# A decoder block in hi/lo fp32r: matmuls of the row-wise products and the classical projections in another loop order

## The chip, the cores and the metric

The kernel runs on one core of a Trainium2 chip. Times are device microseconds (us) of whole executions; the kernel before took 2509.76 us, the median of three (2505.5 to 2514.46). The profile is of one execution on the same core. Its engines are TensorE (PE; the loading of a matmul's stationary operand is shown apart, as PEld), VectorE (DVE), ScalarE (ACT), GpSimd (POOL) and SyncE (SP); all run their own instruction streams in a fixed order and wait for each other by semaphores.

## The reference

One layer of a decoder, 512 tokens of width 2048, all in float32. What matters here are its matrix products:

```python
h = rmsnorm(x, g_mix[l])
z = jnp.einsum('bsd,dc->bsc', h, w_in[l])
cb, cc, cv, q, k, v, f_logit, gate_c, gate_a = jnp.split(z, SPLIT_POINTS, axis=-1)
conv_branch = jnp.einsum('bsc,cd->bsd', cb * causal_dwconv(cc * cv, conv_w[l]), w_conv_out[l])
...                                  # attn: forgetting attention of q, k, v
attn_branch = jnp.einsum('bsc,cd->bsd', attn, w_attn_out[l])
merged = gc * conv_branch + ga * attn_branch        # gates: sigmoids of z's last columns
x = x + jnp.einsum('bsd,de->bse', merged, w_mix_out[l])
h = rmsnorm(x, g_mlp[l])
u = jnp.square(jax.nn.relu(jnp.einsum('bsd,df->bsf', h, w_ff1[l])))
x = x + jnp.einsum('bsf,fd->bsd', u, w_ff2[l])
return rmsnorm(x, g_final)
```

The widths: conv and attention 1024 each, the MLP 8192 (FF1: 2048 to 8192, FF2: 8192 to 2048).

## The kernel before

**Numbers.** Each float32 operand of a large product is written as hi + lo, both of type fp32r, which TensorE reads in one pass. A product is three matmuls, hi x hi, hi x lo and lo x hi. Activations are split once and kept. Weights are split as they come: `split` (L99 to L101) makes the hi part on ScalarE (L100, tile `th`) and the lo part as source minus hi on VectorE (L101, tile `tl`). `th` and `tl` have two buffers each, so that a third `th` can only be written when the matmuls that read the first are through.

**Seven products.** The projections of w_in, FF1 and FF2 cut both operands in 2 x 2 blocks and form seven products (A11, A12, S4, S2, S3, S1, A22) instead of eight, from sums and differences of blocks; these are made by `sub` (L104) and `add` (L107) on VectorE. One product, called a piece here, is a chain of matmuls that accumulate in PSUM. There are two helpers for a piece. `mm_cols` (L126) has the weights as stationary and the tokens as moving operand (FF1, the gates, conv and k/q columns); it isn't touched. `mm_rows` (L148) has the activations as stationary operand `Sx(q)` (hi and lo) and the weights' `hi`, `lo` as the moving one. Its result is two blocks of 128 tokens, b = 0 and 1, in two PSUM banks (for the 256 columns of `gV0`, the two halves of one). It is used by the v heads (`gV0`, `gV1`) and by FF2.

**FF2** is `unit` (L957): 8 segments of the 8192 rows times 2 column groups, so 16 units, each of 7 pieces of 24 matmuls 128x512 (4 values of q, 2 blocks, 3 matmuls). Four weight tiles are loaded, called y00, y01, y11, y10. The pieces come in the order A11 (y00), S3, S2, A22, S1, A12, S4. In between VectorE makes y00 = y01 - y00 and y01 = y11 - y01 (the operand of S3), t2 = y11 - y00 (of S2), t2 = y10 - t2 (of A22); and `into` adds each finished result into `x1` (L107; in the last segment the final result goes through `finish`, L938 and L941, and `residual`, L951). The PSUM tiles a and d change places from one unit to the next.

**The classical projections** are not cut in that way. `gemm_t` (L294) has weights as stationary operand, four result tiles of 128 columns in four banks, and is called for w_conv_out and w_attn_out for each of four column groups; its `consume` (L652 and following) multiplies by the gates and splits the merged sum. `gemm_n` (L315) has tokens stationary and makes w_mix_out; per token tile three matmuls by `mm3` (L310); its `consume` adds the residual (L107) and squares it (L337). Both take the weights in chunks of 4 x 128 rows by `wchunk`, and consume the results after the last chunk.

**What sets the order.** No order is written out by hand: a scheduler takes the program in the order of the code with its dependencies and decides, when the kernel is built, in which order each engine gets its instructions. So a turned loop on TensorE can also shift instructions of VectorE and ScalarE against each other.

In time, the v heads and k/q columns lie up to 277 us, the attention with conv columns up to 505, the gates up to 880, gemm_t from 880 to 1054, gemm_n to 1234, FF1 to 1861, FF2 to 2491, and the last normalisation to 2503.7.

Of the kernel before, what the change touches and what calls it, by code (L numbers as in the profile page):

```python
# [15 lines left out]
P = 128  # L16
# [29 lines left out]
def tile_hybrid_block(ctx: ExitStack, tc, x, g_mix, w_in, b_f, b_gate, conv_w, w_conv_out,  # L46
                      w_attn_out, w_mix_out, g_mlp, w_ff1, w_ff2, g_final, out):
    nc = tc.nc
# [99 lines left out]
    def mm_rows(ps, Sx, hi, lo, first):  # L148

        nq, w = hi.shape[1], hi.shape[2]  # L150
        for b in range(2):
            o = ps[b][:, :w] if len(ps) == 2 else ps[0][:, b * w:(b + 1) * w]
            begin = first and (b == 0 or len(ps) == 2)
            ts = slice(b * P, (b + 1) * P)
            for part in range(2):
                for q in range(nq):
                    Sh, Sl = (e[:, ts] for e in Sx(q))
                    if part == 0:
                        nc.tensor.matmul(o, Sh, hi[:, q, :], start=begin and q == 0, stop=False, skip_group_check=True)  # L159
                        nc.tensor.matmul(o, Sl, hi[:, q, :], start=False, stop=False, skip_group_check=True)  # L160
                    else:
                        nc.tensor.matmul(o, Sh, lo[:, q, :], start=False, stop=q == nq - 1, skip_group_check=True)  # L162

    def moving(t):

# [128 lines left out]
    def gemm_t(view, kt, c0, act, banks, consume, slots=(0, 3, 2)):  # L294

        ps = [bank(i, "pt") for i in banks]
        for k0 in range(0, kt, 4):
            hi, lo = wchunk(view, k0, c0, slot(slots))
            for j in range(4):
                js = slice(j * P, (j + 1) * P)  # L300
                for q in range(4):
                    k = k0 + q
                    xh, xl = act(k)
                    nc.tensor.matmul(ps[j], hi[:, q, js], xh, start=k == 0, stop=False)  # L304
                    nc.tensor.matmul(ps[j], hi[:, q, js], xl, start=False, stop=False)  # L305
                    nc.tensor.matmul(ps[j], lo[:, q, js], xh, start=False, stop=k == kt - 1)
        for j in range(4):
            consume(j, ps[j])

# [5 lines left out]
    def gemm_n(view, kt, c0, act, banks, consume, toks=range(NT), slots=(0, 3, 2), between={}):  # L315

        ps = {t: bank(i, "pn") for t, i in zip(toks, banks)}
        for k0 in range(0, kt, 4):
            hi, lo = wchunk(view, k0, c0, slot(slots))
            for t in toks:  # L320
                for q in range(4):
                    xh, xl = act(k0 + q, t)
                    mm3(ps[t], xh, xl, hi[:, q, :], lo[:, q, :], k0 + q == 0, k0 + q == kt - 1)
            between.get(k0 // 4, lambda: None)()
        for t in toks:
            consume(t, ps[t])
# [754 lines left out]
```

## Time and profile before

| what | value |
|---|---|
| runs | 2505.5, 2509.76, 2514.46 us |
| profiled execution, first to last instruction (span) | 2503.7 us |
| mean granted TensorE clock | 0.996 |
| busy: PE, PEld, DVE, ACT, POOL | 2446.6, 2249.2, 1902.1, 1150.3, 112.7 us |
| matmuls in the profile | 16910 |

The profile shows no own time of its execution beside the span: the span is what a reader compares with the runs, which lie 1.8 to 10.8 us above it, the median 6.1. A matmul's busy time overlaps with the next one's (a 128x512 matmul is shown with 0.39 us), so that the step from one start to the next, not the duration, is what a matmul costs. In a row of a group or of the timeline, `a<-th,us 128*128 128x512` is the result tile, the moving operand and the stationary one, the stationary's shape, and the moving operand's shape. In brackets stands the idle time before an instruction and what ended it. In the rows of stretches come the stretch, its length, each engine's busy time with the number of its instructions, the granted clock, the DMA share and GB/s.

### The profile page before, as it was taken

The page shows a single profiled execution, that of the slowest core. Times are in us where ns is not written, and L with a number is a line of the kernel's source. Part 1 is how long each engine was busy: PE and PEld are TensorE (multiplying, and loading weights), DVE is VectorE, ACT ScalarE, POOL GpSimd, SP SyncE. Part 2 cuts the span into 40 slices and gives each one's busy share as a digit, 9 for nine tenths or more (in the row PEclk, how much of TensorE's full clock was granted, in tenths as well). Part 3 has the DMA queues.
Part 4 walks back from the last instruction along what each step waited for, and adds up shares of the span by engine and source line. Part 5 has one row for each costly group of instructions (what it writes and reads, how often), then busy time and mean ns, then how long its engine had stood idle before and what let it go on. Part 6 is the DMA issues. An engine that isn't in the chain of part 4 may idle for free.

```text
span 2503.7 us, 39010 instructions
## 1 busy us (share of the span) xinstructions
PE 2446.6 (98%) x16910; PEld 2249.2 (90%) x16910; DVE 1902.1 (76%) x1498; ACT 1150.3 (46%) x1136; POOL 112.7 (5%) x184
## 2 busy tenths in 40 slices
PE   7999999999999999999999999999999999999997
PEld 7999989999999988888899999999998878787785
DVE  7877677788777743535688898898887887878888
ACT  6443433434544622235655666666664333333343
POOL 0000000000000000000000000000011000000010
PEclk9999999999999999999999999999999999999999
DMA  7554444456544544435655655646688557664573
GB/s 240 165 170 156 151 135 148 143 179 209 157 134 131 189 161 151 141 121 197 210 172 180 238 178 202 241 174 217 224 308 281 162 189 239 212 215 157 187 259 105
DMA packets 289919, 465.06 MB, mean 186 GB/s; under 512 B 10236, under 2 KB 194644, under 8 KB 289620
## 3 DMA queue, kind: packets, MB, share of 16 engines
q1 hardware_dynamic: 260704, 330.40, 41.1%
q0 software_dynamic: 28176, 131.08, 14.0%
q8 instruction: 132, 2.16, 0.4%
q10 hardware_dynamic: 868, 1.10, 0.1%
q14 instruction: 39, 0.32, 0.0%
HBM read 370.26 MB, written 92.27 MB: 185 GB/s over the span
## 4 chain that ended last, share of the span: by engine, by line
PE 67%; DVE 10%; ACT 3%; DMA 2%; issue 2%; POOL 0%; SPq 0%; ACTq 0%; POOLq 0%; DVEq 0%
PE a L142 5%; PE a L146 5%; PE a L144 5%; PE d L142 3%; PE d L144 3%; PE d L146 3%; DVE tl L101 3%; ACT th L100 3%; PE a L159 3%; PE a L160 3%; PE a L162 3%; PE pt L304 2%; PE pt L305 2%; PE pn L311 2%; PE pn L312 2%; PE pn L313 2%
## 5 line engine op out<-in xcount | busy, mean ns | idle before, releaser
L101 DVE TENSOR_TENSOR tl<-x,th 128x2048 fp32r<-128x2048 f32 (+1 forms) x252 | 575.1, 2288 | 211.0 <-ACT th L100 194.5
L100 ACT ACTIVATE th<-x 128x2048 fp32r<-128x2048 f32 (+1 forms) x252 | 482.4, 1917 | 484.9 <-PE a L144 171.3
L104 DVE TENSOR_TENSOR x<-x,x 128x2048 f32<-128x2048 f32 (+1 forms) x144 | 329.2, 2286 | 17.0 <-DMA x<-in_w_ff_dram 9.3
L100 ACT ACTIVATE th<-y 128x2048 fp32r<-128x2048 f32 x80 | 153.7, 1921 | 271.8 <-DVE y L104 102.6
L101 DVE TENSOR_TENSOR tl<-y,th 128x2048 fp32r<-128x2048 f32 x80 | 182.7, 2284 | 47.4 <-ACT th L100 47.4
L101 DVE TENSOR_TENSOR tl<-raw,th 128x2048 fp32r<-128x2048 f32 x40 | 91.7, 2293 | 151.9 <-ACT th L100 151.4
L159 PE MATMUL a<-th,us 128*128 128x512 f32 x512 | 200.8, 392 | 2.5 <-ACT o L864 1.5
L160 PE MATMUL a<-th,us 128*128 128x512 f32 x512 | 199.4, 389 | 0.0
L142 PE MATMUL a<-ST,th 128*128 128x256 f32 x768 | 178.7, 278 | 8.5 <-ACT th L100 8.5
L144 PE MATMUL a<-ST,th 128*128 128x256 f32 x768 | 178.1, 278 | 0.0
L100 ACT ACTIVATE th<-raw 128x2048 fp32r<-128x2048 f32 x40 | 76.7, 1918 | 175.4 <-PE pt L305 71.5
L142 PEld LDWEIGHTS a<-ST,th 128*128 128x128 f32 x768 | 145.3, 189 | 9.4 <-ACT th L100 9.3
L144 PEld LDWEIGHTS a<-ST,th 128*128 128x128 f32 x768 | 145.3, 189 | 0.0
L142 PE MATMUL a<-S,th 128*128 128x256 f32 x576 | 134.6, 279 | 5.0 <-ACT th L100 5.0
L162 PE MATMUL a<-tl,us 128*128 128x512 f32 x512 | 136.9, 389 | 0.1
L144 PE MATMUL a<-S,th 128*128 128x256 f32 x576 | 134.0, 278 | 0.0
L159 PEld LDWEIGHTS a<-th,us 128*128 128x128 f32 x512 | 96.1, 188 | 27.5 <-ACT th L100 6.1
L142 PE MATMUL d<-ST,th 128*128 128x256 f32 x512 | 117.7, 276 | 0.0
L144 PE MATMUL d<-ST,th 128*128 128x256 f32 x512 | 117.7, 276 | 0.0
L162 PEld LDWEIGHTS a<-tl,us 128*128 128x128 f32 x512 | 95.9, 188 | 20.7 <-DVE tl L101 0.9
L142 PEld LDWEIGHTS a<-S,th 128*128 128x128 f32 x576 | 108.3, 188 | 6.3 <-ACT th L100 6.0
L160 PEld LDWEIGHTS a<-th,us 128*128 128x128 f32 x512 | 96.1, 188 | 19.6
(284 smaller groups left out, 6232.4 us busy)
## 6 DMA issues: line engine op xcount, KB each, us to landing
x<-in_w_in_dram SPq DMA_DIRECT2D x86, 1024.0 KB, 5.8
x<-in_w_ff_dram SPq DMA_DIRECT2D x66, 1024.0 KB, 8.3
y<-in_w_ff_dram SPq DMA_DIRECT2D x64, 1024.0 KB, 6.3
us<-s_d POOLq DMA_DIRECT2D x48, 1024.0 KB, 8.8
s_d<-rh POOLq DMA_DIRECT2D x32, 896.0 KB, 5.3
s_d<-r POOLq DMA_DIRECT2D x32, 896.0 KB, 8.0
raw<-in_w_mix_out_dram SPq DMA_DIRECT2D x24, 1024.0 KB, 5.1
g_d<-o SPq DMA_DIRECT2D x32, 256.0 KB, 2.2
```

The costliest lines, as they stand in the source:

```text
L100: nc.scalar.activation(out=hi, in_=src, func=AF.Copy)
L101: nc.vector.tensor_tensor(out=lo, in0=src, in1=hi.bitcast(F32), op=ALU.subtract)
L104: nc.vector.tensor_tensor(out=out, in0=a, in1=b, op=ALU.subtract)
L142: nc.tensor.matmul(o, hi[:, q, js], Sh, start=first and q == 0 and j == 0, stop=False, skip_group_check=True)
L144: nc.tensor.matmul(o, hi[:, q, js], Sl, start=False, stop=False, skip_group_check=True)
L146: nc.tensor.matmul(o, lo[:, q, js], Sh, start=False, stop=q == nq - 1, skip_group_check=True)
L159: nc.tensor.matmul(o, Sh, hi[:, q, :], start=begin and q == 0, stop=False, skip_group_check=True)
L160: nc.tensor.matmul(o, Sl, hi[:, q, :], start=False, stop=False, skip_group_check=True)
L162: nc.tensor.matmul(o, Sh, lo[:, q, :], start=False, stop=q == nq - 1, skip_group_check=True)
L304: nc.tensor.matmul(ps[j], hi[:, q, js], xh, start=k == 0, stop=False)
L305: nc.tensor.matmul(ps[j], hi[:, q, js], xl, start=False, stop=False)
L311: nc.tensor.matmul(ps, xh, hi, start=first, stop=False)
```

## The change

`mm_rows` had the token block b outermost: for a block all hi matmuls (hi weights with both halves of the activations, 8 of them in FF2), then the 4 with the lo weights; then the other block. Now the part (hi, lo) is outermost, then q, and innermost the block: 16 matmuls with the hi weights, which write the two blocks by turns, then 8 with the lo weights. `gemm_t` had the column tile j outermost; now q is, and for each q hi x hi, hi x lo and lo x hi follow each other with the four column tiles (four banks) innermost. `gemm_n` had the token tile outermost; now q is, and in it tokens hi x weights hi, hi x lo, lo x hi with the token tiles innermost. The number of matmuls, of weight loads and of all other instructions is the same. Line numbers behind `mm_rows` grow by 3 (up to `gemm_t`), 1 and 3: what was L162 is L164, L938 is L941, L941 is L944, L951 is L954.

```diff
--- before.py
+++ after.py
@@ -148,18 +148,21 @@
     def mm_rows(ps, Sx, hi, lo, first):
 
         nq, w = hi.shape[1], hi.shape[2]
-        for b in range(2):
-            o = ps[b][:, :w] if len(ps) == 2 else ps[0][:, b * w:(b + 1) * w]
-            begin = first and (b == 0 or len(ps) == 2)
-            ts = slice(b * P, (b + 1) * P)
-            for part in range(2):
-                for q in range(nq):
-                    Sh, Sl = (e[:, ts] for e in Sx(q))
-                    if part == 0:
-                        nc.tensor.matmul(o, Sh, hi[:, q, :], start=begin and q == 0, stop=False, skip_group_check=True)
-                        nc.tensor.matmul(o, Sl, hi[:, q, :], start=False, stop=False, skip_group_check=True)
-                    else:
-                        nc.tensor.matmul(o, Sh, lo[:, q, :], start=False, stop=q == nq - 1, skip_group_check=True)
+        outs = [ps[b][:, :w] if len(ps) == 2 else ps[0][:, b * w:(b + 1) * w] for b in range(2)]
+        blocks = [slice(b * P, (b + 1) * P) for b in range(2)]
+        for part in range(2):
+            for q in range(nq):
+                Sh, Sl = Sx(q)
+                if part == 0:
+                    for b, (o, ts) in enumerate(zip(outs, blocks)):
+                        begin = first and q == 0 and (b == 0 or len(ps) == 2)
+                        nc.tensor.matmul(o, Sh[:, ts], hi[:, q, :], start=begin, stop=False, skip_group_check=True)
+                    for o, ts in zip(outs, blocks):
+                        nc.tensor.matmul(o, Sl[:, ts], hi[:, q, :], start=False, stop=False, skip_group_check=True)
+                else:
+                    for o, ts in zip(outs, blocks):
+                        nc.tensor.matmul(o, Sh[:, ts], lo[:, q, :], start=False, stop=q == nq - 1,
+                                         skip_group_check=True)
 
     def moving(t):
 
@@ -296,14 +299,12 @@
         ps = [bank(i, "pt") for i in banks]
         for k0 in range(0, kt, 4):
             hi, lo = wchunk(view, k0, c0, slot(slots))
-            for j in range(4):
-                js = slice(j * P, (j + 1) * P)
-                for q in range(4):
-                    k = k0 + q
-                    xh, xl = act(k)
-                    nc.tensor.matmul(ps[j], hi[:, q, js], xh, start=k == 0, stop=False)
-                    nc.tensor.matmul(ps[j], hi[:, q, js], xl, start=False, stop=False)
-                    nc.tensor.matmul(ps[j], lo[:, q, js], xh, start=False, stop=k == kt - 1)
+            for q in range(4):
+                k = k0 + q
+                xh, xl = act(k)
+                for w, a, first, last in ((hi, xh, k == 0, False), (hi, xl, False, False), (lo, xh, False, k == kt - 1)):
+                    for j in range(4):
+                        nc.tensor.matmul(ps[j], w[:, q, j * P:(j + 1) * P], a, start=first, stop=last)
         for j in range(4):
             consume(j, ps[j])
 
@@ -317,10 +318,12 @@
         ps = {t: bank(i, "pn") for t, i in zip(toks, banks)}
         for k0 in range(0, kt, 4):
             hi, lo = wchunk(view, k0, c0, slot(slots))
-            for t in toks:
-                for q in range(4):
-                    xh, xl = act(k0 + q, t)
-                    mm3(ps[t], xh, xl, hi[:, q, :], lo[:, q, :], k0 + q == 0, k0 + q == kt - 1)
+            for q in range(4):
+                k = k0 + q
+                A = {t: act(k, t) for t in toks}
+                for e, w, first, last in ((0, hi, k == 0, False), (0, lo, False, False), (1, hi, False, k == kt - 1)):
+                    for t in toks:
+                        nc.tensor.matmul(ps[t], A[t][e], w[:, q, :], start=first, stop=last)
             between.get(k0 // 4, lambda: None)()
         for t in toks:
             consume(t, ps[t])
```

Three places of the orders in which the engines get their instructions. First, VectorE at the start of an FF2 unit (here the fourth, from A11's lo part `tl_20959` to S2's lo part `tl_21021`; `a_20731` holds the previous unit's S4, `a_20948` this unit's A11). Before:

```order
L101 TENSOR_TENSOR tl_20959<-y00_20950,th_20958 128x2048
L104 TENSOR_TENSOR y00_20950<-y01_20952,y00_20950 128x2048
L107 TENSOR_TENSOR x1_18493<-a_20731,x1_18493 128x2x512
L104 TENSOR_TENSOR y01_20952<-y11_20954,y01_20952 128x2048
L104 TENSOR_TENSOR t2_21017<-y11_20954,y00_20950 128x2048
L107 TENSOR_TENSOR x1_18493<-a_20948,x1_18493 128x2x512
L101 TENSOR_TENSOR tl_20990<-y01_20952,th_20989 128x2048
L101 TENSOR_TENSOR tl_21021<-t2_21017,th_21020 128x2048
```

Of the change:

```order
L101 TENSOR_TENSOR tl_20959<-y00_20950,th_20958 128x2048
L104 TENSOR_TENSOR y00_20950<-y01_20952,y00_20950 128x2048
L104 TENSOR_TENSOR y01_20952<-y11_20954,y01_20952 128x2048
L107 TENSOR_TENSOR x1_18493<-a_20731,x1_18493 128x2x512
L104 TENSOR_TENSOR t2_21017<-y11_20954,y00_20950 128x2048
L101 TENSOR_TENSOR tl_20990<-y01_20952,th_20989 128x2048
L107 TENSOR_TENSOR x1_18493<-a_20948,x1_18493 128x2x512
L101 TENSOR_TENSOR tl_21021<-t2_21017,th_21020 128x2048
```

The addition of the previous S4 now stands behind the difference y01, and that of A11 behind the lo part of S3.

Second, TensorE in the same unit, from the end of S3's first hi matmuls (`th_20989`) into S2 (`th_21020`). Before:

```order
L160 MATMUL d_20949<-th_20989,us_20719 128x512
L159 MATMUL a_20948<-th_21020,us_20722 128x512
L160 MATMUL a_20948<-th_21020,us_20722 128x512
L159 MATMUL a_20948<-th_21020,us_20722 128x512
L160 MATMUL a_20948<-th_21020,us_20722 128x512
L159 MATMUL a_20948<-th_21020,us_20722 128x512
L160 MATMUL a_20948<-th_21020,us_20722 128x512
L159 MATMUL a_20948<-th_21020,us_20722 128x512
L162 MATMUL d_20949<-tl_20990,us_20719 128x512 x4
L159 MATMUL d_20949<-th_20989,us_20719 128x512
```

Of the change:

```order
L159 MATMUL d_20949<-th_20989,us_20719 128x512 x2
L161 MATMUL d_20949<-th_20989,us_20719 128x512 x2
L159 MATMUL d_20949<-th_20989,us_20719 128x512 x2
L161 MATMUL d_20949<-th_20989,us_20719 128x512 x2
L164 MATMUL d_20949<-tl_20990,us_20719 128x512 x8
L159 MATMUL a_20948<-th_21020,us_20722 128x512 x2
L161 MATMUL a_20948<-th_21020,us_20722 128x512 x2
```

Before, seven hi matmuls of S2 stood between S3's first block's hi matmuls and its lo ones, and S3's second block followed; now S3 runs through, 16 hi and 8 lo matmuls, and S2 follows.

Third, VectorE at the start of the last unit (`a_21623` holds the previous unit's S4, which is finished here). Before:

```order
L101 TENSOR_TENSOR tl_21896<-y00_21887,th_21895 128x2048
L104 TENSOR_TENSOR y00_21887<-y01_21889,y00_21887 128x2048
L938 SCALAR_TENSOR_TENSOR x1_18493<-a_21623,turned_11628,x1_18493 128x512 x2
L104 TENSOR_TENSOR y01_21889<-y11_21891,y01_21889 128x2048
L941 TENSOR_TENSOR x1_18493<-x1_18493,gf_18945 128x512 x2
L107 TENSOR_TENSOR x1_18493<-a_21885,x1_18493 128x2x512
L101 TENSOR_TENSOR tl_21927<-y01_21889,th_21926 128x2048
L104 TENSOR_TENSOR t2_21954<-y11_21891,y00_21887 128x2048
L101 TENSOR_TENSOR tl_21958<-t2_21954,th_21957 128x2048
```

Of the change:

```order
L101 TENSOR_TENSOR tl_21896<-y00_21887,th_21895 128x2048
L944 TENSOR_TENSOR x1_18493<-x1_18493,gf_18945 128x512 x2
L941 SCALAR_TENSOR_TENSOR x1_18493<-a_21623,turned_11628,x1_18493 128x512 x2
L104 TENSOR_TENSOR y00_21887<-y01_21889,y00_21887 128x2048
L944 TENSOR_TENSOR x1_18493<-x1_18493,gf_18945 128x512 x2
L104 TENSOR_TENSOR y01_21889<-y11_21891,y01_21889 128x2048
L107 TENSOR_TENSOR x1_18493<-a_21885,x1_18493 128x2x512
L104 TENSOR_TENSOR t2_21954<-y11_21891,y00_21887 128x2048
L101 TENSOR_TENSOR tl_21927<-y01_21889,th_21926 128x2048
L101 TENSOR_TENSOR tl_21958<-t2_21954,th_21957 128x2048
```

The finishing of the previous S4 stands ahead of both differences now, and S3's and S2's lo parts follow each other behind t2.

## The prediction

> **What bounds the kernel now.** I read the share of each engine first, then the chain of waits, then stretches of time.
>
> ```profile
> core 0: 2503.7 us, clock 0.996
> PE 2446.6 (98%) x16910; PEld 2249.2 (90%) x16910; DVE 1902.1 (76%) x1498; ACT 1150.3 (46%) x1136; POOL 112.7 (5%) x184
> PE 67%; DVE 10%; ACT 3%; DMA 2%; issue 2%; POOL 0%; SPq 0%; ACTq 0%; POOLq 0%; DVEq 0%
> ```
>
> TensorE is the bound, but 13% of the chain is VectorE and ScalarE: in places they make its operands too late. The next view tells where; each row is a stretch, its length, and each engine's busy time with a count.
>
> ```profile
> 880.00:1054.00 174.00, 173.97 (x767) 144.06 (x768) 77.28 (x91) 42.70 (x51) 0.00 (x0) 1.00 0.45 153
> 1054.00:1234.00 180.00, 180.00 (x824) 149.68 (x823) 89.77 (x82) 79.83 (x108) 11.08 (x15) 1.00 0.53 178
> 1976.30:2015.30 39.00, 38.67 (x170) 31.33 (x169) 31.50 (x18) 13.44 (x7) 4.48 (x6) 1.00 0.67 227
> 2015.30:2054.30 39.00, 38.66 (x170) 31.37 (x169) 31.55 (x18) 13.44 (x7) 1.49 (x2) 1.00 0.54 178
> 2405.40:2444.00 38.60, 38.19 (x166) 30.65 (x166) 37.92 (x35) 17.45 (x19) 4.34 (x6) 1.00 0.63 208
> 2444.00:2491.00 47.00, 41.61 (x172) 32.65 (x170) 44.43 (x43) 18.57 (x25) 3.08 (x4) 0.96 0.14 45
> ```
>
> The first row is the conv and attention projections (gemm_t): 768 matmuls of 128x512 in 174.0 us, 0.2266 us each, with no idle TensorE. The second is the mix projection (gemm_n), also without idle. The third and fourth are two units of FF2 in the steady state. A unit is 7 pieces of 24 matmuls: 168 x 0.2266 = 38.07 us if nothing is late, but 39.00 us pass. So 0.93 us is lost per unit. The last two rows are the last two units: there VectorE is busy 37.92 of 38.60 and 44.43 of 47.00 us, so it is the bound.
>
> **Where the 0.93 us goes.** The timeline across one unit's start (start, duration, engine, line, tiles; idle before it in brackets; L159 and L160 read a hi part `th`, L162 a lo part `tl`):
>
> ```profile
> 1969.41 0.39 PE L160 MATMUL b<-th,us 128*128 128x512 f32 x1
> 1969.63 1.07 PE L162 MATMUL b<-tl,us 128*128 128x512 f32 x4
> 1969.83 1.92 ACT L100 ACTIVATE th<-y 128x2048 fp32r<-128x2048 f32 x1 [3.52 <-PE b L160]
> 1970.54 0.39 PE L159 MATMUL a<-th,us 128*128 128x512 f32 x1
> 1971.79 2.29 DVE L101 TENSOR_TENSOR tl<-y,th 128x2048 fp32r<-128x2048 f32 x1 [3.06 <-ACT th L100]
> 1974.11 2.29 DVE L104 TENSOR_TENSOR y<-y,y 128x2048 f32<-128x2048 f32 x1
> 1976.32 1.22 DVE L107 TENSOR_TENSOR x<-a,x 128x1024 f32<-128x1024 f32 x1
> 1977.46 2.28 DVE L104 TENSOR_TENSOR y<-y,y 128x2048 f32<-128x2048 f32 x1
> 1979.66 2.28 DVE L104 TENSOR_TENSOR t<-y,y 128x2048 f32<-128x2048 f32 x1
> 1979.86 1.92 ACT L100 ACTIVATE th<-y 128x2048 fp32r<-128x2048 f32 x1 [8.10 <-DVE y L104]
> 1980.51 1.07 PE L162 MATMUL a<-tl,us 128*128 128x512 f32 x4
> 1981.83 0.50 PE L159 MATMUL d<-th,us 128*128 128x512 f32 x1 [0.25 <-ACT th L100]
> 1982.06 1.92 ACT L100 ACTIVATE th<-t 128x2048 fp32r<-128x2048 f32 x1 [0.28 <-DVE t L104]
> 1983.55 0.39 PE L160 MATMUL d<-th,us 128*128 128x512 f32 x1
> 1984.03 0.50 PE L159 MATMUL a<-th,us 128*128 128x512 f32 x1
> ```
>
> Follow the late operand back. S3's first matmul should start at 1980.51 + 4 x 0.2266 = 1981.42 and starts at 1981.83: 0.41 late. It waited for the hi part made from 1979.86 to 1981.78, that for the difference y01 (L104 from 1977.46), and that stood behind L107 at 1976.32, the addition of the previous unit's last result, which is nothing that S3 needs. The addition cost the chain 1977.46 - 1976.32 = 1.14 us. The chain itself began when A12's last hi read (L160 at 1969.41) gave back a `th` buffer. S2's first hi matmul is late in the same way: 1984.03 instead of 1983.55 + 0.23 = 1983.78, so 0.25. The remaining 0.27 of the 0.93 is the pace of the matmuls right after each stall. The waits from 1975 to 2413 us (total, times, longest) say that it repeats in 12 units, the last of which is the one that VectorE bounds anyway, so that 11 count:
>
> ```profile
> PE d L159 <- ACT th L100: 3.0, 12, 0.3
> DVE x L107 <- PE a L162: 22.2, 11, 2.0
> ```
>
> **The change part by part.** The number of matmuls and weight loads stays; only their order moves. Bank alternation by itself I price at nothing: at 1969.63 four matmuls of b are followed by one of a, another bank, at 1970.54, 0.91 us for four, 0.2275 each, as within a bank. Bounds: 0 by this row; what the pace could be otherwise is a rival below.
>
> *FF2, units 3 to 13.* Two things happen to the chain. A `th` buffer now has its last read at the 16th of 24 matmuls, not the 20th: 4 x 0.2266 = 0.91 us earlier. And in the order built for the change VectorE runs y00, y01 and only then the L107. I call T the moment at which the previous S4 gives TensorE over to A11 (above 1981.42 - 24 x 0.2266 = 1975.98). A12 then starts at T - 10.88, its hi reads end at T - 7.25; hi of A11 to T - 5.3, its lo to T - 3.0 (2.28), y00 to T - 0.8, y01 to T + 1.4, hi of S3 to T + 3.4 (1.92). S3 is due at T + 24 x 0.2266 = T + 5.44: 2 us spare. Later: L107 to T + 2.7; t2 (L104) to T + 5.0; lo of S3 from T + 5.4, when its buffer is certainly free, to T + 7.6, due after S3's 16 hi matmuls at T + 9.07; L107 of A11 to T + 8.8; hi of S2 is there by T + 7 and due at T + 10.88; lo of S2 to T + 11, due at T + 14.5. No wait remains on TensorE, and a unit takes 38.07. VectorE's 31.5 us fit in it. Gain: 11 units x 0.93 = 10.2 us; bounds 4.5 (only S3's 0.41 goes) and 10.2. If the cover is wrong by 2 us, the 0.41 stays.
>
> *Last unit.* VectorE sets it:
>
> ```profile
> 2448.25 1.40 DVE L938 SCALAR_TENSOR_TENSOR x<-a,turned,x 128x512 f32<-128x512 f32 x2
> 2453.90 0.50 PE L159 MATMUL d<-th,us 128*128 128x512 f32 x1 [3.70 <-ACT th L100]
> 2460.65 2.29 DVE L101 TENSOR_TENSOR tl<-t,th 128x2048 fp32r<-128x2048 f32 x1 [2.06 <-ACT th L100]
> 2468.35 0.50 PE L159 MATMUL d<-th,us 128*128 128x512 f32 x1 [1.44 <-ACT th L100]
> 2491.06 1.40 DVE L938 SCALAR_TENSOR_TENSOR x<-a,turned,x 128x512 f32<-128x512 f32 x2
> ```
>
> The finishing work (L938, L941) stays ahead of y01, so S3's 3.7 us stall stays but for about 0.5 by the earlier buffer. After it VectorE's one long idle, 2.06 us at 2460.65, closes: the buffer that S2's hi part waited for is free earlier and the lo parts of S3 and S2 now run in one go; and the 1.44 us stall at 2468.35 shrinks. By the same kind of chain, the last L938 comes 34.4 us after S3's start, not 2491.06 - 2453.90 = 37.16: 2.75 us. Sum 3.25; bounds 0 and 5.2 (3.70 + 1.44).
>
> *First units of FF2 (0 to 2).* The one late start that I found there:
>
> ```profile
> 1868.23 0.39 PE L160 MATMUL d<-th,us 128*128 128x512 f32 x1
> 1868.65 1.21 PE L162 MATMUL d<-tl,us 128*128 128x512 f32 x4
> ```
>
> 1868.65 - 1868.23 - 0.23 = 0.19 us, before a lo part. With 16 hi matmuls ahead of the lo ones it goes, and as much in the pace behind it: 0.4; bounds 0 and 0.4.
>
> *gemm_t and gemm_n.* No idle, so nothing to win. All four results of a column group come at its end and are then consumed in a row on VectorE and ScalarE, where they were spread over the last piece before. These are busy 77 and 90 of 174 and 180 us, so they have the room; the first bank must be clear when the next column starts there. I take 0; bounds 0 and a loss of 2 us (a consume delayed by one L101, 2.28).
>
> *v heads and attention.* mm_rows makes the v heads too; there the matmuls run without idle, and the scheduler moves a few instructions of the attention behind them:
>
> ```profile
> 216.00:272.00 56.00, 56.00 (x477) 56.00 (x476) 35.99 (x24) 21.81 (x22) 0.00 (x0) 1.00 0.52 163
> 277.00:505.00 228.00, 223.37 (x1781) 207.45 (x1781) 167.59 (x238) 89.46 (x119) 0.21 (x2) 1.00 0.43 137
> ```
>
> The second row has 4.6 us of idle that could grow or shrink. I take 0, bounds -2 and +2.
>
> **Sum:** 10.2 + 3.25 + 0.4 = 13.9 us. The span becomes 2503.7 - 13.9 = 2489.8. The runs before were 2505.5 to 2514.46, median 2509.76, which is 6.06 above the profiled span; with the same 6.06 the time is 2495.8 us (-0.56%).
>
> **The rivals.** 0.3% of this kernel, about 7.5 us, is what a measurement can tell from no change.
>
> *The alternation quickens the matmuls.* A row of the attention is the nearest evidence on pace:
>
> ```profile
> 299.20 1.02 PE L544 MATMUL sc<-kT,qT 128*128 128x512 f32 x2
> 300.28 0.38 PE L545 MATMUL sc<-cparts,sel 96*128 96x512 bf16 x1
> 300.50 0.22 PE L546 MATMUL sc<-maskb,identb 128*128 128x128 bf16 x1
> ```
>
> 512 columns in bf16 took 300.50 - 300.28 = 0.22 us, less than 0.2266. If the difference came from writing one bank again and again, 2688 + 768 + 768 = 4224 matmuls would gain 4224 x 0.0066 = 28 us, and with the waits 42: 2468 us. Against it: this row writes the same bank as its neighbours too, so the bank isn't what holds fp32r back. The Trainium skill (TensorE: Matmul & The Clock Gate, section Back-to-back issue gap) gives N/2.4 + 2.5, 215.8 ns for 512 columns; from it I estimate 46 us instead of 28, and 2450 us.
>
> *A slower pace takes hold.* The 256-wide matmuls show two paces with TensorE busy throughout:
>
> ```profile
> 555.00:620.00 65.00, 65.00 (x555) 65.00 (x554) 53.18 (x43) 30.99 (x29) 0.30 (x3) 1.00 0.72 228
> 650.00:715.00 65.00, 65.00 (x576) 65.00 (x575) 47.80 (x27) 32.00 (x33) 0.00 (x0) 1.00 0.42 132
> ```
>
> 65/555 = 117.1 ns against 65/576 = 112.8: 3.8% at a full clock. If the turned order puts the 512-wide matmuls into the slow pace, 4224 x 0.2266 = 957 us grow by up to 36 us, less the 13.9: 2532 us. It decides, giving slower by over 7.5 us, once 21.4 / 36 = 60% of them are slow. For it: two stretches with the same instructions differ in nothing but how they follow on each other, and this is what the change turns. Against it: 512-wide rows show it for a few matmuls after a stall only (the seven steps from 1981.83 to 1983.55 take 1.72 us, 0.246 each), and the stretches of gemm_t and FF2 hold 0.2266 to 0.2275.
>
> *The clock falls.* If TensorE were idle a little at each change of bank and the clock fell to the 0.96 of the row at 2444, the 957 us would become 997: 40 - 13.9 = 26 us more, 2536. Against it: the clock is 1.00 in all other rows above, single bank changes included; only the stall of 3.7 us has lowered it, and the change adds none. The Trainium skill (TensorE: Matmul & The Clock Gate, section A second HAM failure mode: psum-queue depth-cycling) tells of such a kernel, which cycled through banks at N=512 and lost clock in the small idle between its groups.
>
> *Nothing to be measured.* The gain is lost again in other moved instructions, above all in the attention and the consuming of gemm_n, or VectorE's next instruction is late by as much: from half of the 13.9 left to a loss of half of it, 2503 to 2517.
>
> **How the numbers follow.** Waits go: 0.66. Nothing measurable: 0.18. Slow pace: 0.07. Lower clock: 0.02. Quicker matmuls: 0.07. Faster takes the first and the last, less 0.03 for a forecast that lands at its lower bound (4.5 + 0 in FF2): 0.70; same 0.18 + 0.03 = 0.21; slower 0.07 + 0.02 = 0.09. The forecast's own range: the bounds of its terms sum to 4.5 - 4 = 0.5 at worst and 10.2 + 5.2 + 0.4 + 2 = 17.8 at best, so 2492 to 2509; widened at the fast end for scatter of the runs of some us, 2487 to 2509. It leaves out the quicker and the slow matmuls, the lower clock and a piece of the case without a difference (above 2509, some 0.04): 0.2 together.
>
> **What would show it.** Right: a unit of FF2 takes 38.1 us in the rows of stretches; the waits of PE d L159 for L100 are gone there; on VectorE the two L104 stand together ahead of L107; gemm_t and gemm_n last 174 and 180 us; the last L938 comes 34 to 35 us after S3's start. Wrong: a 174 us stretch that becomes 169 (banks matter) or 181 (slow pace), a wait at the lo parts in FF2, or new idle from 277 to 505 us that eats the gain.

## The result and the profile after

The change takes 2490.15 us (median of four runs, 2488.25 to 2493.55) against 2508.39 us of the kernel before in the same comparison: 18.2 us less. The ratio of the runs is 0.9933, its 95% interval 0.9916 to 0.995, so the gain lies between 12 and 21 us. Forecast were 2495.8 us, 13.9 us less than the median of before.

The page of the change: span and clock, the engines' busy time, and the chain that ended last.

```profile
core 0: 2486.4 us, clock 0.996
PE 2436.8 (98%) x16910; PEld 2250.5 (91%) x16910; DVE 1898.7 (76%) x1498; ACT 1146.3 (46%) x1136; POOL 112.3 (5%) x184
PE 68%; DVE 8%; DMA 4%; issue 2%; ACT 2%; SPq 0%; POOL 0%; POOLq 0%; DVEq 0%; ACTq 0%
```

VectorE's and ScalarE's part of the chain fell from 13 to 10%. The span is 2503.7 - 2486.4 = 17.3 us shorter; the executions behind the two profiles took 2505.5 and 2488.25 us, 1.8 us more than their spans each. Stretches of the change (stretch, length, busy time and count of each engine, clock, DMA share, GB/s): gemm_t, gemm_n, the fourth unit of FF2, the last but one, and the last one from its first matmul to its last L941.

```profile
875.27:1049.45 174.18, 174.18 (x768) 144.27 (x769) 69.60 (x82) 41.08 (x46) 0.00 (x0) 1.00 0.45 152
1049.45:1229.86 180.41, 180.41 (x824) 149.69 (x823) 93.18 (x91) 80.22 (x113) 11.06 (x15) 1.00 0.53 178
1972.55:2010.63 38.08, 38.08 (x169) 31.53 (x168) 31.64 (x18) 13.33 (x7) 4.47 (x6) 1.00 0.68 229
2391.43:2429.51 38.08, 38.08 (x169) 31.53 (x168) 38.01 (x33) 17.57 (x19) 4.33 (x6) 1.00 0.68 221
2429.51:2474.24 44.73, 40.04 (x169) 32.37 (x167) 44.18 (x47) 19.30 (x26) 3.07 (x4) 0.96 0.14 47
```

gemm_t and gemm_n last as long as before. A unit of FF2 takes 38.08 us, TensorE is busy all the time, and its 168 matmuls step by 0.2267. The timeline at the unit that begins at T = 1972.55 shows how (the `x2` row is two instructions in a row, y00 and y01):

```profile
1965.50 1.92 ACT L100 ACTIVATE th<-y 128x2048 fp32r<-128x2048 f32 x1 [3.52 <-PE b L161]
1969.78 4.62 DVE L104 TENSOR_TENSOR y<-y,y 128x2048 f32<-128x2048 f32 x2
1974.31 1.22 DVE L107 TENSOR_TENSOR x<-a,x 128x1024 f32<-128x1024 f32 x1
1974.51 1.93 ACT L100 ACTIVATE th<-y 128x2048 fp32r<-128x2048 f32 x1 [7.09 <-DVE y L104]
1975.45 2.28 DVE L104 TENSOR_TENSOR t<-y,y 128x2048 f32<-128x2048 f32 x1
1977.99 0.62 PE L159 MATMUL d<-th,us 128*128 128x512 f32 x2
```

A11's hi part starts at T - 7.05 (before: T - 6.15), right after A12's last hi read. y00 and y01 follow each other up to T + 1.85, S3's hi part is there at 1976.44, and S3 starts on time at 1977.99, with 1.55 us to spare. No wait of TensorE stands in FF2 between 1970 and 2400 us.

Where the 17.3 us are, by the starts of the stages in the two traces: FF2 and what follows 14.35 us (units 3 to 13: 10.36; unit 14: 1.30; units 0 to 2: 0.55; the last unit up to its last L941: 1.73; the rest behind it: 0.41), and all that lies ahead of FF2 2.88 us. Only the first two terms come out alike in all profiles of the change, of FF2 alone and of hi first (the experiments below): in a second profile of the same kernel ("The change once more") units 0 to 2 took 115.31 instead of 114.34 us and the last unit 45.86 instead of 44.72, so that FF2 and what follows was 12.27 us shorter than before, not 14.35.

The 2.88 us ahead of FF2 are not a gain of the turned order. In the change the v heads even gained two late starts, because a hi part comes too late (before, the first was missing and the second was 0.79 us):

```profile
87.39 0.51 PE L159 MATMUL c<-th,S 128*128 128x256 f32 x2 [0.91 <-ACT th L100]
94.81 0.50 PE L159 MATMUL a<-th,S 128*128 128x256 f32 x2 [1.49 <-ACT th L100]
```

That is 1.6 us of new waits. They drown in the scatter of what lies ahead of FF2, which the last section shows.

### The profile page after: what moved, and what is told of

Its sections match the earlier page's. It is cut to its first block, busy times and chain, and to the rows that moved or that the text cites. A ratio compares the mean times of both kernels' runs of the same rounds, so it can differ in the third digit from the quotient of the medians.

```text
span 2486.4 us, 39025 instructions
## 1 busy us (share of the span) xinstructions
PE 2436.8 (98%) x16910; PEld 2250.5 (91%) x16910; DVE 1898.7 (76%) x1498; ACT 1146.3 (46%) x1136; POOL 112.3 (5%) x184
## 4 chain that ended last, share of the span: by engine, by line
PE 68%; DVE 8%; DMA 4%; issue 2%; ACT 2%; SPq 0%; POOL 0%; POOLq 0%; DVEq 0%; ACTq 0%
PE pn L326 7%; PE pt L307 7%; PE a L142 5%; PE a L144 5%; PE a L146 4%; PE a L159 4%; PE a L164 4%; PE a L161 4%; DVE tl L101 3%; PE d L144 3%; PE d L142 3%; PE d L146 3%; PE d L159 2%; PE d L161 2%; PE d L164 2%; DMA x<-in_w_ff_dram 2%
## 5 line engine op out<-in xcount | busy, mean ns | idle before, releaser
L159 PE MATMUL a<-th,us 128*128 128x512 f32 x512 | 157.7, 389 | 1.5 <-ACT o L867 1.5
L161 PE MATMUL a<-th,us 128*128 128x512 f32 x512 | 157.6, 389 | 0.0
L326 PE MATMUL pn<-th,m 128*128 128x512 f32 x512 | 134.4, 391 | 0.0
L307 PE MATMUL pt<-act,th 128*128 128x512 f32 x512 | 126.6, 389 | 1.0 <-DVE o L107 1.0
L164 PE MATMUL a<-tl,us 128*128 128x512 f32 x512 | 126.4, 389 | 0.0
L159 PEld LDWEIGHTS a<-th,us 128*128 128x128 f32 x512 | 96.0, 188 | 21.6 <-ACT o L867 1.6
L307 PEld LDWEIGHTS pt<-act,th 128*128 128x128 f32 x512 | 96.0, 188 | 21.0 <-issue 1.2
```

What stands on the lines that cost most here:

```text
L159: nc.tensor.matmul(o, Sh[:, ts], hi[:, q, :], start=begin, stop=False, skip_group_check=True)
L161: nc.tensor.matmul(o, Sl[:, ts], hi[:, q, :], start=False, stop=False, skip_group_check=True)
L164: nc.tensor.matmul(o, Sh[:, ts], lo[:, q, :], start=False, stop=q == nq - 1, skip_group_check=True)
L307: nc.tensor.matmul(ps[j], w[:, q, j * P:(j + 1) * P], a, start=first, stop=last)
L326: nc.tensor.matmul(ps[t], A[t][e], w[:, q, :], start=first, stop=last)
```

## The experiments

**FF2 alone, and all but FF2.** In the first kernel FF2 calls the turned function and the v heads, gemm_t and gemm_n stay as before; the second is its complement.

```diff
+    def mm_ff2(...)            # the turned mm_rows in one kernel, the one of before in the other
-            mm_rows((ps[:, 0], ps[:, 1]), ST[n], hi, lo, first)
+            mm_ff2((ps[:, 0], ps[:, 1]), ST[n], hi, lo, first)
```

> Only FF2's pieces run in the turned order; the v heads, gemm_t and gemm_n stay as before. Theory (waits at the start of an FF2 unit go): units of FF2 take 38.08 us as in the change, the last L938/L941 result comes 616 us after FF2's first matmul instead of 630, and the time falls by 14 us, to 2494. Rival (the rest of the change carries the gain): FF2 keeps 39.0 us per unit and the time stays at 2505 to 2508.

> The v heads, gemm_t and gemm_n turned, FF2 as before. Theory: FF2 keeps 39.0 us per unit; the v heads lose up to 1.7 us (a new wait of 1.1 us ahead of S4's hi part and 0.7 more ahead of S2's), gemm_t and gemm_n lose under 1 us, attention and the pace of the 256-wide matmuls give or take 3: 2504 to 2510. Rival (banks matter in gemm_t and gemm_n): their 1536 matmuls take 11 to 17 us less and the time is 2492 to 2497.

FF2 alone: 2490.37 us against 2507.73, ratio 0.9922 (0.9907 to 0.9937). All but FF2: 2507.14 us, ratio 0.9997 (0.9984 to 1.0011), so that up to 4 us either way could hide there. A unit of FF2 in the first:

```profile
2050.12:2088.20 38.08, 38.08 (x169) 31.53 (x168) 31.65 (x18) 13.33 (x7) 4.47 (x6) 1.00 0.68 229
```

and in the second a unit, gemm_t and gemm_n:

```profile
2053.16:2092.16 39.00, 38.67 (x170) 31.38 (x168) 31.56 (x18) 13.44 (x7) 4.48 (x6) 1.00 0.67 224
879.32:1055.12 175.80, 175.80 (x769) 145.37 (x769) 69.61 (x82) 41.06 (x46) 0.00 (x0) 0.99 0.46 151
881.00:882.00 1.00, 1.00 (x4) 0.81 (x3) 0.00 (x0) 1.00 (x2) 0.00 (x0) 0.50 1.04 357
1055.12:1235.51 180.39, 180.39 (x824) 149.67 (x823) 93.20 (x91) 80.20 (x113) 11.06 (x15) 1.00 0.53 178
```

Here gemm_t is 1.6 us longer than the 174.20 of before: TensorE stood idle for 1.84 us ahead of it, and from about 880.5 to 883.9 us it had half the clock (0.50 in the second of the three rows). In the change's first profile the idle there was 1.02 us and the clock stayed at 1.00. The two new waits of the v heads are there as well (1.06 us, and 1.50 instead of 0.79). The gain that can be measured is FF2's alone; the v heads and the classical projections give none. FF2 alone measured 17.4 us faster, more than its own units and what follows explain (13.7 us in its profile); what is left over lies ahead of FF2, where the code is that of before, and is put down to scatter.

**Hi first without alternation, and alternation without hi first.** Both alter FF2 only; gemm_t, gemm_n and the v heads are as before.

```diff
 # hi first: 8 hi into one bank, 8 into the other, 4 lo, 4 lo
+        for part in range(2):
+            for b in range(2):
+                for q in range(nq): ...
 # alternation: 8 hi, 4 lo, 8 hi, 4 lo, neighbours in different banks
+        for qs in (range(0, nq // 2), range(nq // 2, nq)):
+            for part in range(2):
+                for q in qs:
+                    for e, w in ((Sh, hi), (Sl, hi)) if part == 0 else ((Sh, lo),):
+                        for b in range(2): ...
```

> FF2 alone: all 16 hi matmuls of a piece first, but block after block (8 into one bank, 8 into the other), then 4 and 4 lo ones; no alternation. VectorE's and ScalarE's orders are those of the run that turns FF2 alone. Theory (only the hi-first order counts): units of 38.08 us, the same time as that run within 1.5 us. Rival (neighbours in different banks count): units fall back toward 39.0 us, 2505 to 2508.

> FF2 alone: neighbouring matmuls write the two banks by turns, but hi and lo alternate by halves (8 hi, 4 lo, 8 hi, 4 lo), so that a lo part is due after 8 matmuls and a hi buffer comes free after 20, as before; on VectorE y01 already stands ahead of the L107, as in the change. If the L107 between y00 and y01 was the whole cause: units of 38.1 to 38.3 us. If S2's matmuls, put ahead of S3's lo ones, are what is late: S3 starts on time, S2's hi part is there at T + 8.0 and wanted at T + 7.25, so the wait moves from S3 to S2 and a unit keeps 38.9 to 39.1 us, time 2505 to 2508. If banks count: 38.08 us or less.

Hi first: 2492.85 us, ratio 0.9937 (0.9917 to 0.9957). Alternation: 2506.96 us, ratio 0.9995 (0.9985 to 1.0004). One sentence of the second expectation was mistaken: in the trace of that kernel VectorE has the L107 between y00 and y01, as in the kernel before. So it is before with nothing altered but the alternation. A unit under hi first:

```profile
2055.48:2093.56 38.08, 38.08 (x170) 31.53 (x168) 31.65 (x18) 13.33 (x7) 4.49 (x6) 1.00 0.68 227
```

A unit under alternation alone:

```profile
2052.29:2091.30 39.01, 38.70 (x170) 31.38 (x169) 31.55 (x18) 13.45 (x7) 4.49 (x6) 1.00 0.67 224
```

and TensorE's waits in that kernel from 1974 to 2412 us (total, times, longest):

```profile
PE d L173 <- ACT th L100: 2.9, 12, 0.3
```

Alternation brings nothing: the unit and the wait of S3 are those of before. All of the gain is there without it. (Hi first was 2.5 us slower than the turned FF2, more than the 1.5 expected; in the traces its units 1 to 14 take the same 38.08 us, and the difference lies ahead of FF2 and in its first unit.)

**The place of the L107 on VectorE.** An edge between two VectorE instructions, without a semaphore, holds them in a given order. In the first kernel, TensorE's order is that of before and the L107 stands behind y01; in the second, TensorE's order is that of the change and the L107 stands between y00 and y01; the third is the second with one more edge, which keeps A22's t2 ahead of the next L107.

```diff
+    def behind(late, early):
+        tc.add_manual_dep(late.ins, early.ins.name, ...)    # order alone
 # first (on before): the addition of S4 is issued in the next unit
-        into(0, 1, a, True)
+        pending.append(lambda: into(0, 1, a, True))
+        ...behind(added[0], y01)
 # second (on the change)
+            behind(y01, prev)         # prev: the L107 of the previous unit's S4
+            behind(t2s, y01)
 # third: in addition
+            behind(added[0], t2b)     # the L107 of S3's result behind A22's t2
```

> The kernel before, with one thing altered: on VectorE the addition of the previous unit's S4 (L107) stands behind y01, as in the change; TensorE's order is that of before. If that L107 was the cause (the step of the prediction): S3's 0.41 us goes and a unit takes 38.3 to 38.6 us, 5 to 8 us in all, 2500 to 2503. Theory now (what TensorE does next matters): S3 starts on time, but seven of S2's hi matmuls stand 8 matmuls behind it, their hi part hangs on y00, L107, y01 and t2 whatever the order of these four, and is there no earlier: S2 then waits 0.7 to 0.8 us instead of 0.25, a unit keeps 38.9 to 39.1 us and the time 2505 to 2509.

> The change, with one thing put back: on VectorE the L107 of the previous S4 stands between y00 and y01, as before. If its place was the cause: S3 waits 0.4 us and more and S2 too, a unit takes 38.8 to 39.0 us and the time is 2500 to 2504. Theory now (the 16 hi matmuls ahead are what helps): y01 ends at T + 3.8, its hi part at T + 5.8, S3 waits 0.3 to 0.4 us and nothing after it does; a unit takes 38.4 to 38.6 us, 4 to 6 us more than the change in all, 2494 to 2497.

> As the run with L107 between y00 and y01 under the turned order, but with the second displacement undone that this one brought (the L107 of S3's result ahead of A22's operand t2, which cost a wait of 0.5 us before A22). Theory (the place of the first L107 costs S3's wait alone): S3 waits 0.28 us again, A22 does not; with the pace behind the stall a unit takes 38.4 to 38.5 us, the time is 4 to 5 us above the change: 2494 to 2497. Rival (hi-first alone brings nothing): units stay at 39.1 us, 2506.

The first: 2508.51 us, ratio 1.0009 (0.9994 to 1.0024). The second: 2506.67 us, ratio 0.9996 (0.998 to 1.0013), not the 2494 to 2497 that were expected. The third: 2496.21 us, ratio 0.9944 (0.9922 to 0.9966). A unit of the first:

```profile
2052.62:2091.76 39.14, 38.38 (x170) 31.46 (x168) 31.65 (x18) 13.45 (x7) 4.48 (x6) 1.00 0.66 224
```

and its waits of TensorE from 1975 to 2413 us:

```profile
PE a L159 <- ACT th L100: 9.1, 12, 0.8
```

S3 no longer waits, but S2 does, 0.76 us each: its seven hoisted matmuls come 8 matmuls after S3's first, and their hi part hangs on the same four VectorE instructions in whatever order. The unit is no shorter. A unit of the second:

```profile
2054.24:2093.38 39.14, 38.69 (x170) 31.39 (x169) 31.64 (x17) 13.32 (x7) 4.47 (x6) 1.00 0.64 215
```

and the late start of A22 in it:

```profile
2071.49 0.73 PE L159 MATMUL d<-th,us 128*128 128x512 f32 x2 [0.33 <-ACT th L100]
```

S3 starts 0.28 us late, close to what was expected, but A22 starts 0.50 us late too (0.33 us of idle and a longer first step), which wasn't: the scheduler had also put the L107 of S3's result, which must wait for S3, ahead of A22's t2. In the third that is undone. A unit of it:

```profile
2052.61:2091.10 38.49, 38.38 (x170) 31.46 (x168) 31.64 (x17) 13.32 (x7) 4.47 (x6) 1.00 0.66 225
```

and the timeline at its start:

```profile
2052.81 1.22 DVE L107 TENSOR_TENSOR x<-a,x 128x1024 f32<-128x1024 f32 x1 [0.68 <-PE a L164]
2056.23 1.98 PE L164 MATMUL a<-tl,us 128*128 128x512 f32 x8
2058.32 0.73 PE L159 MATMUL d<-th,us 128*128 128x512 f32 x2
```

S3 is due at 2056.23 + 8 x 0.2267 = 2058.04 and starts 0.28 later; with the pace behind it the L107's place costs 38.49 - 38.08 = 0.41 us per unit, of the 39.02 - 38.08 = 0.94 that a unit of before loses. VectorE stands idle 0.68 us for it, because S4 hasn't ended when its turn comes.

**One piece back.** The change with A12, the last piece but one of a unit, in the order of before; the other six run hi first.

```diff
-            mm_rows((ps[:, 0], ps[:, 1]), ST[n], hi, lo, first)
+            mm = mm_blocks if n == "A12" else mm_rows       # mm_blocks: mm_rows of before
+            mm((ps[:, 0], ps[:, 1]), ST[n], hi, lo, first)
```

> The change, with the one piece A12 (the last but one of a unit) back in the order of before, so that its hi buffer comes free after 20 matmuls instead of 16; the other six pieces run 16 hi matmuls first. Theory (the release of this buffer 0.91 us earlier is the lever: it lets y00 end before S4 does, and the scheduler then puts y01 ahead of the L107): VectorE is back in the order L107, y01; S3 waits 0.4 us or more, A22 some 0.5, a unit takes 39.0 to 39.4 us and the time is 2505 to 2510. Rival (what helps is that the lo parts and S2 are due later, in the other pieces): 38.1 to 38.5 us, 2490 to 2496.

2509.12 us, ratio 0.9997 (0.9979 to 1.0015): one piece in seven takes the gain away. A unit:

```profile
2059.49:2098.74 39.25, 38.67 (x170) 31.38 (x168) 31.55 (x18) 13.32 (x7) 4.47 (x6) 1.00 0.64 215
```

and the timeline at its start:

```profile
2053.34 1.92 ACT L100 ACTIVATE th<-y 128x2048 fp32r<-128x2048 f32 x1 [4.43 <-PE b L179]
2057.62 2.29 DVE L104 TENSOR_TENSOR y<-y,y 128x2048 f32<-128x2048 f32 x1
2059.83 1.22 DVE L107 TENSOR_TENSOR x<-a,x 128x1024 f32<-128x1024 f32 x1
2065.34 0.73 PE L159 MATMUL d<-th,us 128*128 128x512 f32 x2 [0.24 <-ACT th L100]
```

A11's hi part again starts at T - 6.15 (2059.49 - 2053.34), y00 ends 0.4 us after T instead of 0.5 us before it, when the previous result is about ready to be added, and y01 stands behind the L107 again, as before. S3 is 0.41 us late and A22 0.50. That the release of the buffer and the order go together is shown by this run; that the scheduler chose by what was ready first is the likely reason, but the times by which it decides are not on record.

**The last unit.** Two kernels tried to shorten it. In one, the multiplication by the final gain goes to GpSimd; in the other, the finishing of the previous S4 stands behind y00 and y01.

```diff
-                nc.vector.tensor_tensor(out=xs, in0=xs, in1=gf[:, c * S:(c + 1) * S], op=ALU.mult)
+                nc.gpsimd.tensor_tensor(out=xs, in0=xs, in1=gf[:, c * S:(c + 1) * S], op=ALU.mult)
 # the other: finish of (0, 1) of the last segment's first unit is issued in the next unit
+            for i in done:
+                behind(i, y01)
```

> The change, with the multiplication by the final gain (L944, 14 of 0.68 us on VectorE in the last two units) on GpSimd. Theory (VectorE sets the last two units): 9.6 us of its work go; S3's wait in the last unit falls from 4.8 to about 2.3 us, and the last L941 comes 2 to 5 us earlier; the time falls by 2 to 5 us against the change, to 2485 to 2488. Rival: GpSimd takes several us for each, what it multiplies last stands in the way of its final square roots, or it slows VectorE: no gain or a loss.

> The change, with the finishing of the last but one unit's S4 (L941, L944) put behind y00 and y01 of the last unit on VectorE. Theory (VectorE, busy 43.95 of the last 44.5 us, sets the end): S3 starts 2.6 us earlier, T + 7.6 instead of T + 10.2, but the waits come back at later pieces; from the last unit's start to the last L941 it is 44.7 us as in the change, within 1 us. Rival (S3's wait of 4.8 us is the loss): the end comes 2.6 us earlier, 42.1 us, and the time falls to 2488.

GpSimd: 2496.18 us, ratio 0.9961 (0.9949 to 0.9974); the change itself, run beside it, 2492.27, ratio 0.9949 (0.9931 to 0.9968). The two intervals overlap, so a loss isn't proven by the times, but the gain of 2 to 5 us is absent. The timeline says why:

```profile
2428.07 6.46 POOL L944 TENSOR_TENSOR x<-x,gf 128x512 f32<-128x512 f32 x2 [2.98 <-ACT junk L340]
2430.12 3.26 DVE L104 TENSOR_TENSOR y<-y,y 128x2048 f32<-128x2048 f32 x1
2434.62 2.27 DVE L104 TENSOR_TENSOR y<-y,y 128x2048 f32<-128x2048 f32 x1
2434.93 6.39 POOL L944 TENSOR_TENSOR x<-x,gf 128x512 f32<-128x512 f32 x2 [0.40 <-ACT junk L340]
2436.82 3.35 DVE L104 TENSOR_TENSOR t<-y,y 128x2048 f32<-128x2048 f32 x1
```

A multiplication took up to 3.2 us on GpSimd (0.68 on VectorE), and while it ran two of VectorE's three subtractions took 3.26 and 3.35 us instead of 2.28; the third, at 2434.62, did not. At the end VectorE also waited 1.87 us for a square root of GpSimd (L336) that queued behind a multiplication, and only then came to the last L941: the last unit up to it took 50.76 us, against 44.72 and 45.86 in the two profiles of the change.

y01 first: 2492.55 us, ratio 0.9952 (0.9923 to 0.9982), no different from the change. From the last unit's start to the last result it is 46.63 us, 1.9 more than in the first profile of the change and 0.8 more than in the second, which neither theory expected. The stretch:

```profile
2440.42:2487.05 46.63, 41.05 (x169) 32.17 (x167) 44.41 (x47) 19.02 (x26) 3.08 (x4) 0.96 0.12 41
```

and the late starts of TensorE in it, from the timeline:

```profile
2448.25 0.73 PE L159 MATMUL d<-th,us 128*128 128x512 f32 x2 [2.22 <-ACT th L100]
2456.62 0.73 PE L159 MATMUL a<-th,us 128*128 128x512 f32 x2 [1.02 <-ACT th L100]
2464.91 0.73 PE L159 MATMUL d<-th,us 128*128 128x512 f32 x2 [2.24 <-ACT th L100]
```

S3's wait fell from 4.60 to 2.22 us, and S2 and A22 now wait 1.02 and 2.24. VectorE has 44.41 us of work in there; with that much, an earlier S3 alone doesn't bring the end forward, and this order leaves VectorE idle elsewhere (2.2 us here, 0.55 in the first profile of the change).

**The change once more.**

> The change itself, beside the others: 2490 within 2 us. Its FF2 units take 38.08 us again; the 256-wide matmuls up to 650 us and from 1240 us on may be in the slow pace (118 ns) in other stretches than in the first profile, by which the spans differ by some us. If the pace were set by the program's order alone, the same stretches would be slow.

2492.27 us, just outside the 2 us around 2490 that were expected, and units of 38.08 us again. The last unit, with the same orders on all engines, took 1.1 us more than in the first profile:

```profile
2431.72:2477.58 45.86, 41.17 (x169) 33.18 (x167) 44.34 (x46) 19.30 (x26) 3.07 (x4) 0.93 0.12 43
2440.00:2448.00 8.00, 6.08 (x15) 4.82 (x16) 7.97 (x5) 3.78 (x2) 0.00 (x0) 0.57 0.01 2
```

The same 8 us around S3's start in the first profile:

```profile
2438.00:2446.00 8.00, 6.29 (x21) 5.08 (x22) 7.96 (x5) 3.57 (x2) 0.00 (x0) 0.79 0.01 2
```

In both, S3 starts 10.20 us after the unit, behind 4.60 us of idle. The granted clock then is at half for some 7 us here and for some 3.4 us there, which goes with 15 against 21 matmuls in 8 us. Units 0 to 2 differ by another 1 us (a wait of 0.66 us at S1 of the first unit). So the last unit and the first are known to no better than about 1 us. What the run shows of the pace stands in the last section. No version was found that beats the change.

## Why the prediction was right

The direction, the place and the main mechanism were right: 13.9 us were forecast, all of them in FF2, and FF2 with what follows became 14.35 us shorter in the first profile and 12.27 in the second. That the sum came so close is in part luck: a term of 1.30 us was left out, one was 1.5 us too large, and 0.41 us came behind the last L941 without being forecast. The time itself, 2490.15 us, came 5.65 us below the forecast of 2495.8 and below 2492, the best that the bounds of the terms allowed; only the widening to 2487 for scatter covers it. Of the 5.65 us, 3.4 are the span (2486.4 against 2489.8: 0.45 in FF2 and behind it, 2.88 ahead of it), and 2.3 the distance of the median from the span, 3.75 instead of 6.06. The last two of these are scatter between executions, as far as the runs show. Point by point:

- **Units 3 to 13.** Forecast 38.07 us per unit and 10.2 us in all; measured 38.08 and 10.36. The chain from A12's hi reads to S3 ran as worked out, 0.2 to 0.5 us later (y01 at T + 1.85 instead of T + 1.4), and 1.55 us of the 2 us to spare were left. This term came out the same in six profiles: the change twice, FF2 alone, hi first, and the two kernels on the last unit.
- **The account of the cause** was right only as a whole. It gave two things: the buffer that comes free 0.91 us earlier, and the L107 that no longer stands ahead of y01. The runs show that they go together: turning back A12 alone brings the L107 back and the whole loss with it. And the L107's 1.14 us, which the prediction put in the middle of S3's delay, isn't a price that can be saved by itself: moving only the L107 takes S3's wait away and gives S2 0.76 us of it. It needs S3's 16 hi matmuls ahead of S2's as well. With these in place the L107's position is worth 0.41 us per unit of the 0.94; the other 0.53 is what hi first gives with the L107 in its old place, once A22's t2 is kept ahead of the next one (the third kernel with edges).
- **Unit 14** was counted as bound by VectorE (37.92 of 38.60 us) and priced at nothing. That was the term left out. The stretch read there was 0.78 us shorter than the unit; the whole unit of before is

```profile
2405.22:2444.60 39.38, 38.97 (x169) 31.30 (x168) 38.70 (x35) 17.45 (x19) 4.34 (x6) 1.00 0.63 208
```

  It went from 39.38 to 38.08, 1.30 us. A stretch with VectorE busy 98% had been read as its bound, while TensorE's waits there were those of the other units (0.93 us with the pace behind them) and one more before S4's lo part (0.37). VectorE's work fitted: 38.01 us of it into 38.08, with some moved on into the last unit.
- **The last unit** was mis-sized: 3.25 us forecast, 1.73 measured in the first profile and 0.60 in the second. S3's wait was to shrink by 0.5 and grew. In the change VectorE, a view of the start of its last unit shows, runs an L944 pair and the L941 pair ahead of y00 and the second L944 pair ahead of y01:

```profile
2429.45 1.28 DVE L944 TENSOR_TENSOR x<-x,gf 128x512 f32<-128x512 f32 x2
2430.66 1.40 DVE L941 SCALAR_TENSOR_TENSOR x<-a,turned,x 128x512 f32<-128x512 f32 x2
2431.97 2.28 DVE L104 TENSOR_TENSOR y<-y,y 128x2048 f32<-128x2048 f32 x1
2434.17 1.28 DVE L944 TENSOR_TENSOR x<-x,gf 128x512 f32<-128x512 f32 x2
2435.38 2.28 DVE L104 TENSOR_TENSOR y<-y,y 128x2048 f32<-128x2048 f32 x1
2439.71 1.22 PE L159 MATMUL d<-th,us 128*128 128x512 f32 x2 [4.60 <-ACT th L100]
```

  y01 ends at T + 8.15 and S3 starts at T + 10.2; before it was T + 9.3. The order was known; the step that put S3 0.5 us earlier by the buffer's release overlooked that the chain no longer hung on that buffer. The other half held in the first profile, where the last L941 starts 2474.24 - 2439.71 = 34.5 us after S3, as forecast (34.4), and VectorE's idle of 2.06 us is gone; in the second, with the longer stretch of half clock, it is 35.7 us, so that the agreement to 0.1 us was luck.
- **gemm_t, gemm_n** at nothing: 174.18 and 180.41 us, against 174.20 and 180.11. **The v heads and attention** at nothing within 2 us: all but FF2 gave a ratio of 0.9997. The 1.6 us of new waits in the v heads, shown above, are inside that bound, but were not foreseen in it.
- **The first units** hit their 0.4 us by chance (0.55): in the second profile they took 0.42 us more than before. The late lo parts of before are gone in both.
- **Quicker matmuls** did not come: the step stayed 0.2267 us wherever neighbours wrote different banks. The Trainium skill (TensorE: Matmul & The Clock Gate, section Back-to-back issue gap) would have 0.2158 for a matmul by itself, not for a stream like this one; no run here showed a sustained step under 0.2266 for this kind.
- **The slow pace** did not take hold of the 512-wide matmuls, and the **clock** did not fall through the turned order in the change: 1.00 in gemm_t, gemm_n and 15 units of FF2; in the last unit 0.96 in the first profile, as before, and 0.93 in the second. What the same page tells in its section A second HAM failure mode: psum-queue depth-cycling (the Trainium skill) did not occur in these units of FF2, where TensorE has no idle between banks and the granted clock is 1.00.

## What to carry to other kernels

Where a hi and a lo part come from a buffer pair, read every hi matmul first: it gives the buffer back earlier and makes the lo part due later, and the two together can let an engine's chain pass a point where one instruction more or less stands ahead of it. When a stall hangs on a chain of four instructions, ask before you reorder them who waits for the last: moving one ahead only moves the wait, unless the next reader is due later too. Turning loops for the sake of PSUM banks alone brought nothing here. And before a term is called hit, profile the same kernel twice: the last unit here moved by 1.1 us from one execution to the next.

## What the runs showed of the hardware

**Two paces.** The 256-wide matmuls run at 113 ns or at 117 ns with a full clock and TensorE busy throughout, and which of the two a stretch gets changes from one execution to the next. The change in its first profile:

```profile
550.00:650.00 100.00, 100.00 (x885) 100.00 (x884) 83.07 (x61) 48.18 (x47) 0.30 (x3) 1.00 0.67 211
1500.00:1600.00 100.00, 100.00 (x871) 99.92 (x871) 85.29 (x64) 61.34 (x63) 5.28 (x10) 1.00 0.57 201
```

and the same kernel in the second profile:

```profile
1500.00:1600.00 100.00, 100.00 (x885) 100.00 (x884) 86.34 (x65) 63.12 (x65) 5.33 (x10) 1.00 0.59 208
```

871 against 885 matmuls in the same 100 us, with TensorE busy all the time: 1.6%. In the kernel with A12 turned back it is the other stretch that is slow:

```profile
550.00:650.00 100.00, 100.00 (x858) 100.00 (x857) 79.26 (x57) 47.61 (x41) 0.30 (x3) 1.00 0.66 207
```

By the traces FF2 began between 1856.9 and 1868.9 us in the 13 profiles. What is computed ahead of it has one of two loop orders: with the turned one it began at 1861.5 us in the mean of eight profiles, with the one of before at 1860.6 in the mean of five. The scatter of 12 us is nearly as large as the gain, and the 2.88 us ahead of FF2 lie inside it and can't be credited to the change. That the pace makes most of this scatter is not shown, and what sets the pace stays open.

**GpSimd beside VectorE.** While GpSimd multiplied 128x512 tiles, two of VectorE's 128x2048 subtractions went from 2.28 to 3.26 and 3.35 us, and four of the 14 GpSimd multiplications took 3.2 us where the last two, near the end of the program, took 1.26 and 1.28. Not every overlap cost time, and why is open.

**Half clock after an idle TensorE.** Behind the 4.60 us of idle in the last unit the granted clock went to half in both profiles of the change, for some 3.4 us in one and some 7 in the other; behind 1.84 us of idle ahead of gemm_t it did so in one profile, behind 1.02 us at the same place in another it did not.

**A schedule that flips** (no matter of the hardware). Turning back one piece of seven, which moves the release of its buffer by 0.91 us, changed the order of two VectorE instructions, and with it came waits of 0.41 us at S3 and 0.50 us at A22 in each unit.
